# A decoder trunk's stages reordered across the two halves, with FFN operands and split mixer weights passed through DRAM

## Chip, core and metric

The kernel runs on one core of a Trainium2 chip. The time is the device time of one execution in microseconds, the median of several runs; lower is better. TensorE is shown as PE, VectorE as DVE, ScalarE as ACT, GpSimd as POOL, SyncE as SP.

## What is computed

One layer on a sequence of 2048 positions of width 1024, everything in float32:

```python
h = rmsnorm(x, norm_mix)
z_pool, z_cv, z_cg, z_u, z_v, z_gate = split(h @ w_in)      # 5632 columns
y_a = pool_mixer(z_pool)          # causal means over 2, 4, 8, 16 positions, then 128x256 products
y_b = conv_module(z_cv, z_cg)     # causal depthwise conv of 31 taps, layernorm, silu, product
y_c = sgu_mixer(z_u, z_v)         # gelu, layernorm, product along 128-position chunks, product
g = sigmoid(z_gate + b_gate)      # three gates of width 1024
x = x + (g0 * y_a + g1 * y_b + g2 * y_c) @ w_out
h = rmsnorm(x, norm_ffn)
a, val = split(h @ ffn_up)        # 2 x 2816 columns
x = x + (silu(causal_dwconv3(a)) * val) @ ffn_down
out = rmsnorm(x, norm_final)
```

## The kernel before

**Precision.** Every float32 operand of a product is split in two parts: `hi`, a rounded copy made on ScalarE, and `lo = x - hi`, made on VectorE. `mm3` makes three matmuls of 128x128 by 128x512 from them (hi.hi, hi.lo, lo.hi; lines 225 to 227). Nearly all of TensorE's work is this.

**Tiling.** The sequence is cut into four quarters of 512 positions (`NQ = 4`, `T = 512`), channels lie on the partitions, and a tile of one quarter is 128x512, 256 KB. An arena of 67 such tiles (`halves`) holds all data that moves; `half` takes one, `release` gives it back. PSUM has eight banks of 128x512.

**Stages.** Two quarters make a half, and each half runs: mix of its first quarter, mix of its second, the FFN's first product `ffn_up` for both quarters together, `down` of the first, `down` of the second. A mix is `mixers` plus `w_out`, 61 weight chunks and 1476 matmuls. `ffn_up` uses Strassen's scheme with seven products p1 to p7 for each of 22 index values (1848 matmuls): the two quarters and the two halves of the 1024 input channels make a 2x2 matrix of blocks, the gate and value columns of the weight make the other. Its moving operands are a11, a12, s2, s1, s3, a22, s4, each four tile pairs, 56 tiles in all; `first_sums` makes the first two during the last `w_out`, `second_sums` the others as `ffn_up` begins. `up_order` is the order of products by hand. `down` is two passes (`h`) of 22 steps (`k`) of 12 matmuls, each pass over half of the output channels.

**Weights.** `self.seq` lists the weight parts in order of use. `load` brings one from DRAM into `raw` (two buffers of 512 KB) on SP's queue, `ensure` splits it into `whi` and `wlo` (four buffers, `AHEAD = 4`) as soon as a chunk retires, with priority. A chunk serves 24 matmuls. For `ffn_up` the parts are `x1` (the plain block for p1, p2), `t2` and `t3` (differences that GpSimd makes from a pair of blocks in the double tile `both`, line 161) and `b22`.

**Order.** TensorE, SP and GpSimd follow the written order; VectorE and ScalarE are ordered by the framework's scheduler by priority. Each engine works its own list in order. `bg` is a list of small background steps (mostly the 31 taps of the convolution) that `drain` works off between chunks. The `acts` of the FFN and the residual `x1` go to DRAM on ScalarE's queue and come back on SP's; `queue_act` loads an act and splits it, once for each pass of `down`. During the second `down` of the first half the next quarter's x is loaded and its norm made (`next_x`, `norm_cols`).

## Time and profile before

| | us |
|---|---|
| median of 3 runs | 2829.61 (2827.94 to 2830.6) |
| the profiled run | 2830.14 |
| its span, first to last instruction | 2828.4 |
| TensorE busy | 2767.2 |
| VectorE busy | 1978.9 |
| ScalarE busy | 1167.3 |
| GpSimd busy | 424.9 |

Busy time of an engine is time in which at least one of its instructions is in work. Matmuls overlap, so TensorE's busy time says little of its rate; the number of matmuls that begin in a stretch does, together with the clock that was granted (1.00 is 2.4 GHz, 0.50 is 1.2 GHz).

### The profile page before, as it was taken

How to read it: one execution, taken by the hardware profiler on the slowest of the kernel's cores; microseconds unless marked ns; L12 is line 12 of the kernel's file. 1: busy time of each engine (PE TensorE's matmuls, PEld its weight loads, DVE VectorE, ACT ScalarE, POOL GpSimd, SP SyncE). 2: the span in 40 equal slices, each digit the busy share in tenths (PEclk: the TensorE clock that was granted, in tenths of full speed). 3: DMA queues.
4: the chain of work that ended last, by engine and by line, in shares of the span. 5: the costliest groups of instructions: out<-in, count | busy, mean ns of one | idle time of the engine just before them, and what ended most of it. 6: DMA issues, size and time to landing. Idle time of an engine off the chain costs nothing.

```text
span 2828.4 us, 32169 instructions
## 1 busy us (share of the span) xinstructions
PE 2767.2 (98%) x11938; PEld 2231.7 (79%) x11938; DVE 1978.9 (70%) x2980; ACT 1167.3 (41%) x1628; POOL 424.9 (15%) x326
## 2 busy tenths in 40 slices
PE   8999999999899999999999999999998999999998
PEld 7888888888688887787788888888886888877886
DVE  8995889658856565555689857896688556555565
ACT  4434324253544443445434343242534444434443
POOL 1000100000332332000200301000003332330020
PEclk9999999999899999999999999999998999999999
DMA  4224332333133233566432443323332233235564
GB/s 162 90 93 153 112 127 82 104 120 127 57 115 119 90 119 108 175 216 216 171 112 82 143 167 116 120 82 97 127 119 82 90 119 111 98 112 191 204 223 156
DMA packets 130013, 361.13 MB, mean 128 GB/s; under 512 B 14624, under 2 KB 16672, under 8 KB 129856
## 3 DMA queue, kind: packets, MB, share of 16 engines
q1 hardware_dynamic: 109296, 319.60, 33.8%
q10 hardware_dynamic: 18432, 32.51, 3.0%
q0 software_dynamic: 2128, 6.96, 0.6%
q8 instruction: 93, 1.52, 0.2%
q14 instruction: 64, 0.52, 0.1%
HBM read 318.65 MB, written 40.37 MB: 127 GB/s over the span
## 4 chain that ended last, share of the span: by engine, by line
PE 92%; DVE 3%; DMA 2%; POOL 1%; ACT 1%; issue 1%; SPq 0%; DVEq 0%; POOLq 0%; ACTq 0%
PE ps L226 30%; PE ps L227 30%; PE ps L225 30%; DVE h L268 1%; DMA both<-wts 1%; DVE wlo L193 1%; POOL tw L161 1%; DMA h<-act 1%; POOL h L355 0%; DMA h<-xT 0%; ACT whi L192 0%; PE ps L603 0%; ACT h L267 0%; PE ps L305 0%; PE ps L316 0%
## 5 line engine op out<-in xcount | busy, mean ns | idle before, releaser
L225 PE MATMUL ps<-h,whi 128*128 128x512 f32 x3648 | 1442.2, 395 | 27.1 <-ACT h L267 12.1
L226 PE MATMUL ps<-h,whi 128*128 128x512 f32 x3648 | 1442.1, 395 | 19.0 <-DVE h L268 18.5
L227 PE MATMUL ps<-h,wlo 128*128 128x512 f32 x3648 | 1439.0, 394 | 2.0 <-DVE wlo L193 1.9
L225 PEld LDWEIGHTS ps<-h,whi 128*128 128x128 f32 x3648 | 689.3, 189 | 192.1 <-ACT h L267 16.3
L226 PEld LDWEIGHTS ps<-h,whi 128*128 128x128 f32 x3648 | 689.1, 189 | 191.0 <-DVE h L268 33.8
L227 PEld LDWEIGHTS ps<-h,wlo 128*128 128x128 f32 x3648 | 689.9, 189 | 160.8 <-DVE wlo L193 4.2
L192 ACT CAST whi<-raw 128x1024 fp32r<-128x1024 f32 x376 | 394.2, 1050 | 891.0 <-PE ps L226 636.2
L193 DVE TENSOR_TENSOR wlo<-raw,whi 128x1024 fp32r<-128x1024 f32 x376 | 470.2, 1252 | 340.2 <-ACT whi L192 337.7
L444 DVE SCALAR_TENSOR_TENSOR h<-cbuf,params,h 128x512 f32<-128x512 f32 x480 | 340.6, 747 | 2.5
L193 DVE TENSOR_TENSOR wlo<-tw,whi 128x1024 fp32r<-128x1024 f32 x88 | 107.8, 1225 | 309.5 <-ACT whi L192 309.3
L161 POOL TENSOR_TENSOR tw<-both 128x512 f32<-128x512 f32 x88 | 122.9, 1396 | 1239.5 <-DMA both<-wts 1064.7
L268 DVE TENSOR_TENSOR h<-h,h 128x512 fp32r<-128x512 f32 x309 | 228.0, 764 | 68.0 <-ACT h L267 64.6
L267 ACT CAST h<-h 128x512 fp32r<-128x512 f32 x309 | 189.1, 619 | 183.9 <-DMA h<-act 75.3
L192 ACT CAST whi<-tw 128x1024 fp32r<-128x1024 f32 x88 | 92.4, 1050 | 212.7 <-POOL tw L161 119.5
L161 POOL TENSOR_TENSOR tw<-both,tw 128x512 f32<-128x512 f32 x88 | 156.5, 1778 | 3.4
L992 POOL TENSOR_TENSOR h<-h,h 128x512 f32<-128x512 f32 (+1 forms) x32 | 37.4, 1178 | 423.4 <-ACT h L982 422.9
L225 PE MATMUL ps<-whi,h 128*128 128x512 f32 x256 | 101.0, 395 | 0.0
L227 PE MATMUL ps<-whi,h 128*128 128x512 f32 x256 | 100.9, 394 | 0.0
L226 PE MATMUL ps<-wlo,h 128*128 128x512 f32 x256 | 100.7, 393 | 0.0
L355 POOL TENSOR_TENSOR h<-h,h 128x512 f32<-128x512 f32 x24 | 41.1, 1749 | 392.6 <-PE ps L227 375.4
L298 ACT ACTIVATE h<-h 128x512 f32<-128x512 f32 (+1 forms) x99 | 57.4, 609 | 39.1 <-DVE h L955 12.3
L299 DVE TENSOR_TENSOR h<-h,h 128x512 f32<-128x512 f32 (+1 forms) x82 | 58.9, 718 | 12.6 <-ACT h L298 9.5
(147 smaller groups left out, 1678.6 us busy)
## 6 DMA issues: line engine op xcount, KB each, us to landing
raw<-wts SPq DMA_DIRECT2D x376, 512.0 KB, 3.6
both<-wts SPq DMA_DIRECT2D x88, 512.0 KB, 4.5
h<-act SPq DMA_DIRECT2D x176, 256.0 KB, 4.1
act<-h ACTq DMA_DIRECT2D x88, 256.0 KB, 3.0
h<-xT SPq DMA_DIRECT2D x64, 256.0 KB, 5.4
x<-h ACTq DMA_DIRECT2D x32, 256.0 KB, 4.3
h<-x SPq DMA_DIRECT2D x32, 256.0 KB, 5.0
out<-h POOLq DMA_DIRECT2D x24, 256.0 KB, 2.7
```

Of the source, the lines that this page charges most:

```text
L161: sub = lambda o, a, b: self.nc.gpsimd.tensor_tensor(o, a, b, op=ALU.subtract)
L192: nc.scalar.copy(h, src)
L193: nc.vector.tensor_tensor(l, src, h.bitcast(F32), op=ALU.subtract)
L225: mm(out, l[0], r[0], start=start, stop=False)
L226: mm(out, l[0], r[1], start=False, stop=False)
L227: mm(out, l[1], r[0], start=False, stop=stop)
L267: self.nc.scalar.copy(hi, src)
L268: self.nc.vector.tensor_tensor(lo, src, hi.bitcast(F32), op=ALU.subtract)
L298: self.nc.scalar.activation(t, x, AF.Square)
L299: eng.tensor_tensor(s, s, t, op=ALU.add)
L355: nc.gpsimd.tensor_tensor(t, x[k], rstd, op=ALU.mult)
L444: nc.vector.scalar_tensor_tensor(acc, buf[:, k:k + T], w, acc, op0=ALU.mult, op1=ALU.add)
```

## The change

The stages run in another order: mix 0, mix 1, mix 2, `ffn_up` of the first half, `down(0)`, mix 3, `down(1)`, `ffn_up` of the second half, `down(2)`, `down(3)`.

The operands of `ffn_up` are made by a background job, `rows_job`: it loads x1 of both quarters, norms it, makes the seven blocks, splits them and stores them in DRAM. Jobs are generators; `tick` runs one step of each list between chunks, if the arena has room. `fetch_block` brings a block back. `spill` queues a store, which `flush` issues on SP one call later. The stores of acts and x1 go the same way, so none is issued by ScalarE.

The split weights of the mixers are stored in DRAM, those of odd chunks in mix 0 and of even ones in mix 1 (`put`), and from the next mix on the pair `hi`, `lo` is loaded (`get`) in place of the raw chunk and its split. `raw` has three buffers, the double tile is gone, and `b22` is loaded again by itself. `up_order` puts p4 and p3 of an index among the products of the next one. `down` keeps the 22 acts of a quarter, split, in the arena for both passes. The squares for the FFN's norm are added on GpSimd. GpSimd is ordered by the scheduler like VectorE and ScalarE. The final norms of the first three quarters are jobs too.

```diff
-NHALF = 67
-RAW = 2
+NHALF = 69
+RAW = 3
...
+def up_order(first=0, end=NPAIR):
+    out = [(p, first + i) for i in range(LAG) for p in ("p1", "p2")]
+    for i in range(first, end + 1):
+        n = i + LAG - 1 if i > first else end
+        out += [("p6", i), ("p4", i - 1), ("p5", i), ("p1", n), ("p7", i), ("p2", n), ("p3", i - 1)]
+    return [(p, i) for p, i in out if first <= i < end]
...
+        def mix(q):
+            return [(("w", "put", "get")[min(2, max(0, q + i % 2))], i) for i in range(ca)]
+        self.seq = mix(0) + mix(1) + mix(2) + up + down + mix(2) + down + up + down * 2
...
     def load(self):
...
+        elif what == "b22":
+            raw = self.wpool.tile([P, 1024], F32, name="raw", tag="raw", bufs=RAW)[:, 0:T]
+            self.nc.sync.dma_start(out=raw, in_=self.aps["wts"][i + NPAIR][:, T:])
         elif what == "t2":
-            raw = self.wpool.tile([P, 2, 1024], F32, name="both", tag="both", bufs=1)
+            raw = []
             for h in range(2):
-                self.nc.sync.dma_start(out=raw[:, h, :], in_=self.aps["wts"][i + h * NFF])
+                raw.append(self.wpool.tile([P, 1024], F32, name="raw", tag="raw", bufs=RAW))
+                self.nc.sync.dma_start(out=raw[h], in_=self.aps["wts"][i + h * NPAIR])
...
     def ensure(self, ahead=AHEAD):
-            if self.loaded < n and self.loaded - self.prepped < RAW and ahead > 1:
+            if self.loaded < n and self.loaded - self.prepped < 2 and ahead > 1 and not (
+                    self.loaded > self.prepped and self.seq[self.prepped][0] == "t3"):
                 self.load()
...
+                if what == "get":
+                    for t, d in zip((hi, lo), self.cache[i]):
+                        nc.sync.dma_start(out=t.bitcast(F32), in_=d)
+                    self.ready.append((hi, lo))
+                    self.prepped += 1
+                    continue
...
     def take(self, ahead=AHEAD):
         self.ensure(ahead)
+        got = self.ready.popleft()
+        what, i = self.seq[self.taken]
+        if what == "put":
+            for t, d in zip(got, self.cache[i]):
+                self.nc.sync.dma_start(out=d, in_=t.bitcast(F32))
...
+    def tick(self, n=1):
+        for _ in range(n):
+            for jobs in self.jobs:
+                if jobs and self.room() >= self.spare + jobs[0][1]:
+                    self.step(jobs)
...
+    def flush(self, n=1):
+        for _ in range(n):
+            for dst, keys, t, flag in self.due:
+                self.nc.sync.dma_start(out=dst, in_=t)
+                release(keys)
+                if flag:
+                    self.there[flag] = True
+            self.due, self.fresh = self.fresh, []
...
     def next_col(self, h, mid=None, at=(4,), ahead=AHEAD):
         ps = self.col(self.take(ahead), h, mid=mid, at=at)
         self.retire()
+        self.flush()
+        self.tick(self.pace)
...
     def w_out(...):
-            self.nc.scalar.dma_start(out=self.x1[q][j], in_=x1[j])
+            self.add_square(s[1], x1[j], nc.gpsimd, j == 0)
+            self.spill(self.x1[q][j], [keys[j]], x1[j])
...
+    def rows_job(self, st, q0, src, gname, rst, flags):
...
+        while not all(self.there[f] for f in flags):
+            yield 4
+        yield 4
+        kr, r = self.fetch(rst)
+        nxt = self.fetch([src[q][0] for q in (q0, q0 + 1)])
+        yield
+        yield
+        for k in range(H):
+            (k0, k2), (a0, b0) = nxt
+            yield 3
+            norm(a0, k, 0)
+            norm(b0, k, 1)
+            self.block(st, "a11", k, a0)
+            ks, s3 = self.half()
+            g.tensor_tensor(s3, a0, b0, op=ALU.subtract)
...
+            (k3,), (b1,) = self.fetch([src[q0 + 1][k + H]])
+            self.block(st, "s3", k, s3)
...
+            norm(b1, k + H, 1)
+            self.block(st, "a22", k, b1)
+            g.tensor_tensor(b0, b0, b1, op=ALU.add)
+            g.tensor_tensor(b1, b1, s3, op=ALU.subtract)
...
     def down(self, q, last, each, done, tail=None):
             for k in range(n):
-                self.queue_act(q, h, k + AHEAD)
+                if h == 0:
+                    self.queue_act(q, k + 2 * AHEAD)
...
+                if h == 0:
+                    acts[k] = self.queued.pop((q, k))
+                step(w, k, range(F4), slice(0, T), acts[k][1])
+                if h:
+                    release(acts[k][0])
+                    if not last:
+                        self.queue_act(q + 1, k)
...
     def build(self):
+        for q in range(3):
+            rows = next_rows(q + 1) if q < 2 else iter(range(4))
+            self.pace = 1 + (q == 2)
...
+                if q == 2 and got in (1, 2):
+                    self.need("f0")
+                    self.fetch_block("f0", BLOCKS[got - 1])
...
+                if q == 2 and j in (0, 2, 4):
+                    self.fetch_block("f0", BLOCKS[2 + j // 2])
...
+        rows = next_rows(3)
+        def each(h, k):
+            self.tick()
+            if h and k in (1, 6, 12, 16):
+                got["h"] = next(rows)
+        x = self.down(0, True, each, done(0, nc.gpsimd))
...
-        with tc.manual_schedule(engines={mybir.EngineType.PE, mybir.EngineType.SP, mybir.EngineType.Pool}):
+        with tc.manual_schedule(engines={mybir.EngineType.PE, mybir.EngineType.SP}):
```

`need` works off the jobs at once until the blocks named are stored; in the third mix it is called before the last eight products, in `down(1)` at step 10 of the second pass.

## Rows read from the trace of the kernel before

**Rows 1.** The page: busy time by engine; DMA total.
```profile
PE 2767.2 (98%) x11938; PEld 2231.7 (79%) x11938; DVE 1978.9 (70%) x2980; ACT 1167.3 (41%) x1628; POOL 424.9 (15%) x326
DMA packets 130013, 361.13 MB, mean 128 GB/s; under 512 B 14624, under 2 KB 16672, under 8 KB 129856
```

**Rows 2.** Stretches: busy us (starts) of PE, PEld, DVE, ACT, POOL; clock, DMA share, GB/s.
```profile
700.00:760.00 60.00, 49.51 (x184) 35.07 (x183) 55.50 (x84) 30.20 (x45) 21.27 (x13) 0.86 0.13 47
800.00:860.00 60.00, 60.00 (x261) 48.68 (x261) 35.98 (x60) 25.22 (x34) 19.83 (x13) 1.00 0.32 116
1100.00:1180.00 80.00, 75.46 (x315) 59.23 (x314) 43.45 (x67) 31.22 (x43) 12.43 (x8) 0.98 0.44 151
1280.00:1320.00 40.00, 35.91 (x145) 28.37 (x144) 21.49 (x27) 21.60 (x34) 4.72 (x3) 0.91 0.60 210
1360.00:1400.00 40.00, 33.62 (x133) 26.27 (x132) 30.85 (x34) 16.71 (x24) 13.59 (x8) 0.91 0.42 141
2100.00:2160.00 60.00, 49.56 (x184) 35.25 (x183) 53.35 (x74) 27.98 (x43) 26.09 (x16) 0.86 0.20 72
2520.00:2580.00 60.00, 54.95 (x224) 42.25 (x223) 30.73 (x45) 22.73 (x31) 12.47 (x8) 0.97 0.44 146
```

**Rows 3.** The chain that ended last: start us, us, what ran.
```profile
739.10 3.47 DVE h L268 x2
...
1106.43 5.04 DMA both<-wts
1112.99 4.79 POOL tw L161 x3
...
1287.88 5.50 DMA h<-xT
...
1373.09 11.49 POOL h L355 x7
```

**Rows 4.** Groups of instructions: count, busy us, mean ns, idle before and its cause.
```profile
L193 DVE TENSOR_TENSOR wlo<-raw,whi 128x1024 fp32r<-128x1024 f32 x376 | 470.2, 1252 | 340.2 <-ACT whi L192 337.7
L192 ACT CAST whi<-raw 128x1024 fp32r<-128x1024 f32 x376 | 394.2, 1050 | 891.0 <-PE ps L226 636.2 <-issue 120.7 <-PE ps L227 95.7
L268 DVE TENSOR_TENSOR h<-h,h 128x512 fp32r<-128x512 f32 x309 | 228.0, 764 | 68.0 <-ACT h L267 64.6 <-issue 3.1
L267 ACT CAST h<-h 128x512 fp32r<-128x512 f32 x309 | 189.1, 619 | 183.9 <-DMA h<-act 75.3 <-DVE h L652 57.9 <-DVE h L506 12.8
L161 POOL TENSOR_TENSOR tw<-both,tw 128x512 f32<-128x512 f32 x88 | 156.5, 1778 | 3.4
L161 POOL TENSOR_TENSOR tw<-both 128x512 f32<-128x512 f32 x88 | 122.9, 1396 | 1239.5 <-DMA both<-wts 1064.7 <-DVE h L765 102.3 <-DVE h L900 32.0
L782 DVE SCALAR_TENSOR_TENSOR h<-h,params,h 128x512 f32<-128x512 f32 x16 | 11.3, 745 | 0.0
```

**Rows 5.** The page's DMA issues: queue, count, size, median us to landing.
```profile
raw<-wts SPq DMA_DIRECT2D x376, 512.0 KB, 3.6
```

**Rows 6.** Stretches of 20 us with the highest DMA traffic, columns as in rows 2.
```profile
260.00:280.00 20.00, 20.00 (x88) 16.17 (x87) 13.82 (x20) 12.73 (x17) 0.00 (x0) 1.00 0.80 297
...
1260.00:1280.00 20.00, 20.00 (x88) 16.19 (x87) 10.40 (x14) 9.24 (x13) 1.31 (x1) 1.00 0.73 261
...
2720.00:2740.00 20.00, 20.00 (x88) 16.22 (x87) 16.79 (x11) 7.33 (x10) 11.98 (x13) 1.00 0.80 273
```

**Rows 7.** The middle of the second mix, columns as in rows 2.
```profile
380.00:530.00 150.00, 150.00 (x658) 121.98 (x657) 147.32 (x247) 55.20 (x85) 0.00 (x0) 1.00 0.31 99
```

**Rows 8.** Pool copies and products, 40 to 600 us: min/median/max, first and last start.
```profile
L495 ACT COPY h<-ps x8: 572/582/622, 107.1 to 473.2; 128x512 f32<-128x512 f32 x8
...
L506 DVE SCALAR_TENSOR_TENSOR h<-h,h x8: 681/684/687, 110.7 to 482.5; 128x512 f32<-128x512 f32 x8
```

**Rows 9.** SP's waits by cause: us in total, times, longest.
```profile
SPq L150 <- DVE wlo L193: 1474.1, 308, 14.7
```

**Rows 10.** SP in order of time: start us, us, what was issued.
```profile
1287.44 4.72 SPq L371 DMA_DIRECT2D h<-xT  x8
```

## What I expect of the change, before seeing it run

> **What bounds the kernel now.** I read the page's first part first. TensorE is busy for 2767 of 2828.4 us and VectorE for 1979; the DMA engines move 361 MB at a mean of 128 GB/s [rows 1]. So no work taken off VectorE or the DMA engines shortens the run by itself; only time in which TensorE stands still, or is slow, can be won. The busy share hides how much that is, because a matmul counts as busy while it waits for its operands to stream. I therefore counted matmul starts by stretch. A full stretch holds 261 starts in 60 us, 0.230 us each [rows 2]. The reader is to see that the short stretches are few and sit only where one stage hands over to the next: the two entries of the FFN's first product (184 starts in 60 us at a granted clock of 0.86, a mean of 2.4 GHz and half of it), its two ends, and two places in the second `down` of the first half. Between them, for hundreds of microseconds, the rate is full.
>
> The losses, starts missing times 0.230 us [rows 2]: entry of the first FFN, 261 - 184 = 77, 17.7 us; the same at the second, 17.7; end of the first, 348 - 315 = 33, 7.6; of the second, 261 - 224 = 37, 8.5; at 1280, 174 - 145 = 29, 6.7; at 1360, 174 - 133 = 41, 9.4. Together 67.6 us. What follows an idle stretch at a low clock is in these counts.
>
> The chain says what each place waits for [rows 3]. At the FFN's entry VectorE and ScalarE make the operand rows while TensorE waits for each. At the FFN's end it is the load of the next weight pair, then GpSimd's subtractions one after another. At 1287 the x of the next quarter is loaded, and act splits queue behind its squares. At 1373 seven GpSimd products of the next norm come in a row, with act splits behind them on ScalarE.
>
> Outside these places lie the start and the final norm's tail, which the change leaves alone. 2828.4 - 67.6 = 2760.8 us is the span if all six places close and nothing opens.
>
> **The change, part by part.** Matmuls: the counts of `mixers`, `strassen` and `down` are those of before; only some sums for a norm differ, under 1 us. Hence the whole effect lies in stalls.
>
> *FFN entry (gain 35.4, bounds 0 and 35.4).* `rows_job` makes the seven operands during the third mix and during `down(1)`, and they come back by DMA from the a11 block on, some 60 us ahead in the first half. The work does not vanish. Per half it is 16 norm products at 0.745, 28 splits at 0.619 on ScalarE and 0.764 on VectorE, and 16 sums on GpSimd at about 1.6, between its 1.4 and 1.8 [rows 4]: 33 us of VectorE, 17 of ScalarE, 26 of GpSimd, 77 in series. Its cover is 340 us of matmuls in the mix (1476 x 0.230) and 122 in `down(1)`. VectorE was full in the middle of a mix, 147 of 150 us [rows 7]. There, however, 61 weight splits of 1.25 us go (76 us of VectorE, 64 of ScalarE [rows 4]), as the third and fourth mix fetch them ready-made. In all 152 such splits and 88 act splits leave: 190 + 67 us of VectorE and 160 + 54 of ScalarE. That is worth nothing to the end but room.
>
> *FFN end (gain 16.1, bounds 0 and 16.1).* The two tiles of a pair now come from the three `raw` buffers, not from one double tile that stays full until `b22` is split; the next pair can load as soon as t3 is subtracted. A pair of 5.04 us [rows 3], 3.2 us of GpSimd and 2.3 of splits make 10.5 us; without p1 and p2 an index lasts 60 x 0.230 = 13.8 us. I leave 2 us for what still shows.
>
> *Inside the FFN.* t3's split must now wait for p4 of the index before, and p7 uses it two products, 5.5 us, later; before there were four products between them. The split takes 1.05 + 1.25 us [rows 4], leaving 3.2 us for whatever ScalarE and VectorE are in the middle of. Bounds: nothing, or 44 times the whole 2.3 us if nothing of it hides, 101 us; I take nothing, since one running instruction on each, at most about 1 us, fits.
>
> *`down` to mix.* The fourth quarter's norm is made in the second pass of `down(0)`, where acts stay resident: no act is loaded or split there, so the 16.1 us at 1280 and 1360 have no victim. But the norm now starts 6 steps (16.6 us) before the mix, and its eight GpSimd products alone take about 14 us (seven took 11.49 [rows 3]). Bounds 0 and 9.4, the old price of that chain; I take 4.
>
> *DMA.* Bytes go from 361 to about 566 MB: 122 stores of split weights (64 MB), 304 loads of 0.52 MB for 152 of the same (+80), 224 block moves (+59), x1 read again (+13), `b22` again (+12), fewer act loads (-23). Over the run that is 204 GB/s. The third mix carries the peak: 64 MB of weights, 15 of spilled blocks, 11 of fetched ones, about 11 of x, x1 and the rest, 101 MB in 340 us, 297 GB/s. That is just the fastest 20 us of before, 297 GB/s at a DMA share of 0.80 with TensorE at full rate [rows 6]. A weight is asked for three chunks, 16.6 us, ahead and lands in 3.6 for the first 0.5 MB, about 5 for two [rows 5], so some 11 us are in hand. They go in `w_out(2)`: behind the two chunks that retire together stand 2.1 MB of weights and 2.1 of s2, then 3.1 more, then 1.05 for the last chunk. These 8.4 MB take 23.5 us at the 358 GB/s that 261 at a share of 0.73 makes [rows 6], and 2.2 us of landing; the chunk is due 22.1 us after them: 3.6 us late. Bounds 0, and 12 at the bare 261 GB/s; I take 4.
>
> *The SP queue.* x1 and act stores move from ScalarE's queue to SP's, and with them all spills. SP works in order; it already stands waiting much of the time, 1474 us for weight splits on one line [rows 9], which costs nothing because raw loads are issued four to five chunks ahead. Now a spill that waits for a late split holds the next weight. `flush` puts one chunk between making and storing. Eight issues take 4.72 us [rows 10]; the third mix has some 256 (122 halves of weights, 134 of 0.26 MB), so about 151 of 340 us. How late VectorE runs: the eighth pool copy on ScalarE comes 9.3 us before its VectorE product [rows 8], inside the 11 us in hand, less the chunk. Bounds 0 and 154 (below); I take 2.
>
> Sum: 2760.8 + 4 (`w_out`) + 4 (norm) + 2 (FFN end) + 2 (SP) = 2772.8 us of span. The profiled run was 2830.1, 1.7 above its span and 0.5 above the median, so the forecast is 2774.
>
> **The rivals.** *DMA binds the third mix.* The mean of 297 GB/s is the best of before, and stores are mixed in. At 273 GB/s, another stretch at a share of 0.80 [rows 6], it takes 370 us, 30 more; at 261, 387, 47 more. Time 2804 to 2821. For it speaks that demand and best row coincide; against it that 0.80 is not 1.
>
> *The row jobs reach TensorE through SP: slower.* Place: the third mix and `down(1)`. Each spill waits for its split, each fetch for a free half, each norm for its fetch, and the next weight stands behind them on SP. If the 77 us chain of each half came out of the cover whole, it would cost 154 us: 2774 + 154 = 2928. It ends even when 44% of it shows (67.6 of 154), and slower beyond; with half showing, 2851. For it speaks the full VectorE in mid-mix [rows 7]; against it the 76 us of splits that leave that mix.
>
> The Trainium skill (DMA: Bandwidth & Descriptors, Anatomy of one DMA) says that a DMA's semaphore wait is served on the issuing sequencer before the transfer is dispatched, not by the DMA engines. SP's rows of waiting agree [rows 9]; by that rule alone this rival would be the likely one wherever a spill is late.
>
> *t3's slot eats the gain: no change.* If the split is late by 1.3 us at each of the 44 indices, 57 us return: 2774 + 57 = 2831. It begins where ScalarE and VectorE make it wait over 3.2 us. Against it: one instruction each is under that.
>
> **How the numbers follow.** Forecast 0.66, with its own range of 2758 to 2792; DMA-bound mix 0.15; row jobs in SP's way 0.11; t3's slot 0.08. About 0.2%, 5.7 us, is what a measurement of this kernel can tell from no change. Faster by more: 0.66 + 0.15 + 0.02 (t3 at a smaller price) = 0.83. Within: 0.04 of t3 and 0.01 of the row jobs, 0.05. Slower: 0.10 + 0.02 = 0.12. The range runs from 2754, six places closed and the scattered losses a little smaller, to 2820, the DMA-bound mix at its dearer end; the third and fourth cases stay outside, under 0.2.
>
> **What would show it.** Right: 261 starts per 60 us across both FFN entries, at a clock of 1.00; 356 weight splits instead of 508; VectorE near 1710 us, ScalarE near 950, DMA near 566 MB. In `w_out(2)` and at the entry of the fourth mix a wait of a few microseconds each, the first for a weight's DMA, the second for a norm's split. Wrong: TensorE waiting for DMA loads of weights through the third mix (first rival), SP rows waiting for splits ahead of them (second), or one wait per FFN index for the split made from `tw` (third).

## The result, and the profile after

The changed kernel takes 2791.98 us (median of 4 runs, 2789.69 to 2792.74) against 2830.11 us (median of 4, 2827.94 to 2830.63): ratio 0.9865, interval 0.9848 to 0.9882. That is 38 us less. The forecast was 2774, 56 us less; the time lies inside the range given, 18 us above its likeliest value and at the upper edge of the 2758 to 2792 that belonged to the forecast's own case. The profiled execution took 2792.74 us with a span of 2791.0 us, so the accounting below is made against that span.

First the page of the changed kernel, busy time by engine and the DMA total. It answers to [rows 1].

```profile
PE 2753.0 (99%) x11958; PEld 2231.2 (80%) x11958; DVE 1819.1 (65%) x2701; ACT 966.2 (35%) x1390; POOL 446.4 (16%) x363
DMA packets 203456, 566.71 MB, mean 203 GB/s; under 512 B 22784, under 2 KB 24832, under 8 KB 203296
```

The reader is to see that 201 us of ScalarE went, near the 217 that were forecast, but 160 us of VectorE where 269 were (it was put at 1710), and that the bytes are the 566 MB that were counted; none of these says anything of where 38 us came from. For that the starts are counted again by stretch, in the columns of [rows 2]. By the count of its matmuls, the third mix of this kernel runs from 704 to 1056, `ffn_up` of the first half to 1489, `down(0)` to 1612, the fourth mix to 1962, `down(1)` to 2086, and the second `ffn_up` to 2527.

```profile
704.00:1056.00 352.00, 348.66 (x1510) 282.11 (x1510) 218.25 (x364) 81.17 (x138) 37.65 (x23) 1.00 0.81 282
800.00:840.00 40.00, 37.47 (x164) 30.16 (x163) 37.52 (x76) 15.20 (x27) 10.92 (x6) 0.96 0.81 276
1060.00:1100.00 40.00, 37.86 (x163) 30.18 (x162) 24.95 (x41) 17.00 (x23) 15.68 (x12) 0.96 0.60 218
1440.00:1500.00 60.00, 60.00 (x261) 48.75 (x260) 43.28 (x63) 26.32 (x38) 11.61 (x8) 1.00 0.48 160
1489.00:1612.00 123.00, 123.00 (x533) 99.89 (x532) 66.19 (x82) 48.50 (x66) 17.99 (x12) 1.00 0.52 179
1720.00:1760.00 40.00, 38.17 (x166) 30.47 (x165) 39.19 (x75) 13.40 (x23) 0.00 (x0) 0.96 0.37 131
2000.00:2120.00 120.00, 113.47 (x480) 90.87 (x478) 79.21 (x91) 46.36 (x66) 31.72 (x21) 0.97 0.99 363
2080.00:2140.00 60.00, 52.01 (x206) 40.59 (x205) 32.73 (x44) 20.97 (x30) 16.78 (x12) 0.91 0.95 350
2090.00:2120.00 30.00, 23.47 (x91) 17.80 (x89) 19.97 (x28) 12.20 (x18) 11.35 (x8) 0.89 1.04 398
2470.00:2530.00 60.00, 60.00 (x261) 48.60 (x260) 44.20 (x62) 26.10 (x36) 11.77 (x8) 1.00 0.45 147
```

Both FFN ends, at 1489 and 2527, and the whole of `down(0)` now run at the full rate, 0.230 to 0.231 us a start. The first FFN entry (1060) has 163 starts where 174 fit, 2.5 us lost; the second (2080) 206 where 261 fit, 12.7 us. Two new short places stand in the middle of the third and fourth mix: 164 and 166 starts. A stretch like these with 16 small transposes among its matmuls holds 183 when nothing stops it (shown below in a kernel where it does), so 4.4 and 3.9 us are lost.

What TensorE waited for, in total, times, longest:

```profile
PE ps L291 <- ACT whi L208: 8.4, 3, 5.2
PE ps L394 <- DVE rs_y L360: 7.4, 4, 4.4
PE ps L291 <- DVE h L675: 4.4, 3, 2.5
```

Not shown are 7.4 us at the start, where the kernel before waits 6.9, and two small groups of 1.7 and 1.6. The weight split `whi` of line 208 is waited for at the two FFN entries (1.6 and 6.8 us), `h` of line 675 in the middle of the two mixes, and the norm's root `rs_y`, once 4.5 us at the very end, now costs 3.0 us more in three places (0.8, 0.5 and 1.7). No load of a weight is waited for in the third mix.

SP at the second entry, in order of time (start us, us, what was issued), around the first product of `ffn_up` at 2086:

```profile
2067.37 3.99 SPq L285 DMA_DIRECT2D h<-f1a  x8
...
2088.95 1.00 SPq L164 DMA_DIRECT2D raw<-wts  x2
2090.24 12.34 SPq L285 DMA_DIRECT2D h<-f1s  x16
```

The last store of the row job (line 275) goes out at 2065.5. Behind it five groups of eight block tiles of 256 KB (line 285; 10.5 MB in 35 us) stand around the first pair of weights that is to be subtracted (line 164). Sixteen loads take 12.34 us to issue, 0.77 each, where eight took 4.72 before, 0.59 each [rows 10]. The pair issued at 2088.95 reaches GpSimd at 2096.92; its four subtractions, 3 us for two, end at 2102.99, and ScalarE, in whose list other work stands ahead, splits at 2106.73: that is the wait for `whi`.

### The profile page after: what moved, and what is told of

Read it like the earlier page. It is cut to its first block, busy times and chain, and to the rows that moved or that the text cites. A ratio compares the mean times of both kernels' runs of the same rounds, so it can differ in the third digit from the quotient of the medians.

```text
span 2791.0 us, 32498 instructions
## 1 busy us (share of the span) xinstructions
PE 2753.0 (99%) x11958; PEld 2231.2 (80%) x11958; DVE 1819.1 (65%) x2701; ACT 966.2 (35%) x1390; POOL 446.4 (16%) x363
## 3 DMA queue, kind: packets, MB, share of 16 engines
q10 hardware_dynamic: 1152, 1.05, 0.1%
## 4 chain that ended last, share of the span: by engine, by line
PE 93%; DVE 4%; DMA 1%; issue 1%; ACT 0%; POOL 0%; SPq 0%; DVEq 0%; ACTq 0%; POOLq 0%
PE ps L293 31%; PE ps L291 31%; PE ps L292 31%; DVE h L514 2%; DVE h L338 0%; DMA h<-x 0%; PE ps L386 0%; DMA h<-act 0%; DVE wlo L209 0%; DVE h L572 0%; DVE h L548 0%; DMA params<-par 0%; PE ps L394 0%; PE ps L375 0%; DVE h L539 0%
## 5 line engine op out<-in xcount | busy, mean ns | idle before, releaser
L209 DVE TENSOR_TENSOR wlo<-raw,whi 128x1024 fp32r<-128x1024 f32 (+1 forms) x268 | 351.2, 1311 | 291.9 <-ACT whi L208 237.8
L208 ACT CAST whi<-raw 128x1024 fp32r<-128x1024 f32 (+1 forms) x268 | 262.1, 979 | 543.2 <-PE ps L292 387.8
L514 DVE SCALAR_TENSOR_TENSOR h<-cbuf,params,h 128x512 f32<-128x512 f32 x480 | 357.8, 783 | 2.4
L369 POOL TENSOR_TENSOR h<-h,h 128x512 f32<-128x512 f32 x38 | 55.9, 1470 | 1154.1 <-ACT h L368 1153.5
L337 ACT CAST h<-h 128x512 fp32r<-128x512 f32 x219 | 133.7, 620 | 294.7 <-DVE h L858 80.8
L171 POOL TENSOR_TENSOR tw<-raw 128x512 f32<-128x512 f32 x88 | 115.4, 1331 | 591.1 <-DMA raw<-wts 466.5
L338 DVE TENSOR_TENSOR h<-h,h 128x512 fp32r<-128x512 f32 x219 | 163.0, 760 | 70.5 <-ACT h L337 68.8
L701 ACT ACTIVATE h<-ps,params 128x512 f32<-128x512 f32 x96 | 65.7, 687 | 255.6 <-PE ps L293 255.5
L719 DVE TENSOR_TENSOR h<-ps,h 128x512 f32<-128x512 f32 x64 | 44.2, 690 | 163.2 <-PE ps L293 156.1
L171 POOL TENSOR_TENSOR tw<-raw,tw 128x512 f32<-128x512 f32 x88 | 129.4, 1470 | 3.4
L955 DVE TENSOR_TENSOR h<-h,ps 128x512 f32<-128x512 f32 x44 | 30.3, 688 | 130.3 <-ACT h L954 130.3
```

The source lines that it names most:

```text
L171: sub = lambda o, a, b: self.nc.gpsimd.tensor_tensor(o, a, b, op=ALU.subtract)
L208: nc.scalar.copy(h, src)
L209: nc.vector.tensor_tensor(l, src, h.bitcast(F32), op=ALU.subtract)
L337: self.nc.scalar.copy(hi, src)
L338: self.nc.vector.tensor_tensor(lo, src, hi.bitcast(F32), op=ALU.subtract)
L369: eng.tensor_tensor(s, s, t, op=ALU.add)
```

## The experiments

All ratios are against the kernel before, which ran on the same chip. It took 2828.12 to 2829.46 us beside these kernels and 2830.11 beside the changed one, so up to 2.0 us of each difference to the change that is given below belongs to the chips. Against its own runs of the kernel before, the change saves 38.1 us, e1 42.8, e2 41.0, e3 27.3, e5 43.4, e6 39.2, e7 27.3, e9 32.6, e10 55.4, e11 45.0, and e12 loses 0.6. By the intervals only e3, e7, e10 and e12 are clear of the change; for the others the windows of the profiled runs have to decide. How far a window varies by itself can be seen in kernels that leave its place alone: 800 to 840 holds 156 starts in e2, 161 in e6, 173 in e9; 1060 to 1100 holds 163 in e6 and 169 in e2 and e9; 2080 to 2140 holds 206 in the changed kernel, 210 in e5 and 213 in e2.

**e1: spread the traffic at the two entries.** Blocks are fetched some products later, and the x1 of `down(1)` is stored one tile per product, not all at once.

```diff
-            self.fetch_rest("f0", m, (0, 0))
+            self.fetch_rest("f0", m, (3, 8))
...
-        for dst, key, t in zip(self.x1[1], *x):
-            self.spill(dst, [key], t)
+        later_x = {m: (dst, [key], t) for m, (dst, key, t) in enumerate(zip(self.x1[1], *x))}
...
-            self.fetch_rest("f1", m, (0, 2, 8))
+            self.fetch_rest("f1", m, (3, 6, 10))
+            if m in later_x:
+                self.spill(*later_x[m])
```

> The blocks left over at the entry of each FFN product are loaded a few products later (a22 and s4 at products 3 and 8 instead of both at 0; s3, a22, s4 at 3, 6, 10 instead of 0, 2, 8), and the eight stores of x1 at the second entry go out one per product. No work is left out. Theory: TensorE stands still there because 16 to 24 block tiles stand ahead of the weights on SP's queue; the losses of 2.8 and 12.7 us at the two entries fall below 5 together and the time to about 2782. Rival: the second entry is late because the call of need holds SP until the last row spills are made; then the 12.7 us stay within 3 us and the time is 2789 or more.

Measured: 2785.97, ratio 0.9854 (0.9837 to 0.987), 6.0 us below the change, between the 2782 of the theory and the 2789 of the rival. The second entry in e1, columns as in rows 2:

```profile
2075.00:2125.00 50.00, 43.82 (x175) 34.64 (x174) 30.21 (x38) 18.90 (x26) 15.03 (x11) 0.90 0.95 353
```

The first entry is full (262 starts in 1050 to 1110). The second still loses 42 starts of 217, 9.7 us, at a DMA share of 0.95. Spreading what follows 2086 moves some 3 us of the 12.7 at most, as e2 and e5 differ there by 1 to 2 without a change of theirs; most of the loss stays.

**e2: the final norm's job later.** One number, so that the final norm of the first quarter runs later in the fourth mix.

```diff
-        self.add(self.later(4, self.final(0, x, got[0])))
+        self.add(self.later(30, self.final(0, x, got[0])))
```

> The final norm of the first quarter starts 26 chunks later in the fourth mix. No work is left out. Theory: its GpSimd products and DMA issues slow the convolution's taps on VectorE (18 taps took 22.9 us, 12.6 without it), and TensorE pays 4.4 us for that in the middle of the mix; the wait for the gated product's split goes, and the time falls to about 2788. Rival: VectorE is full in the middle of a mix anyway; the wait stays over 3 us and the time at 2791 to 2793.

Measured: 2787.73, 0.9856 (0.9842 to 0.9871); 4.3 us below the change, as the theory had it, and 1720 to 1760 is full. First e2's window, with the 16 transposes in it:

```profile
1720.00:1760.00 40.00, 40.00 (x183) 32.72 (x182) 30.72 (x51) 12.82 (x21) 0.00 (x0) 1.00 0.45 158
```

The cause is in VectorE's order of time, the taps of the convolution (line 514) shortly after the mix begins. In the changed kernel:

```profile
1647.35 16.32 DVE L514 SCALAR_TENSOR_TENSOR h<-cbuf,params,h 128x512 f32<-128x512 f32 x8
```

GpSimd in the same stretch of the changed kernel:

```profile
1647.89 3.05 POOL L1092 TENSOR_TENSOR h<-h,h 128x512 f32<-128x512 f32 x2 [31.24 <-ACT h L1082]
1650.89 1.13 POOL L1093 DMA_DIRECT2D out<-h  x2
1652.03 2.54 POOL L1092 TENSOR_TENSOR h<-h,h 128x512 f32<-128x512 f32 x2
1654.49 1.12 POOL L1093 DMA_DIRECT2D out<-h  x2
```

And VectorE in e2, where GpSimd does nothing there:

```profile
1648.42 10.68 DVE L514 SCALAR_TENSOR_TENSOR h<-cbuf,params,h 128x512 f32<-128x512 f32 x16
```

Eight taps in 16.32 us beside GpSimd, sixteen in 10.68 without: a tap of 0.67 us became 2.04 in the mean. Not all eight are slow. Three last 0.74 us, two 1.78 and three 3.7; here are one of each of the slow kinds:

```profile
1648.01 1.78 DVE L514 SCALAR_TENSOR_TENSOR h<-cbuf,params,h 128x512 f32<-128x512 f32 x1
```

```profile
1651.41 3.71 DVE L514 SCALAR_TENSOR_TENSOR h<-cbuf,params,h 128x512 f32<-128x512 f32 x1
```

The first ends when the GpSimd product beside it does, within 0.2 us. The second begins between two DMA issues of GpSimd and lasts through one issue, two products and the next issue. The 11 us of VectorE lost here are missed 70 us later, where VectorE has no slack (39.19 busy of 40). Whether TensorE feels it depends on the order of VectorE's list: e3 (below) has five such taps too, the longest 3.71 us, and the middle of its fourth mix is full.

**e5: the first row job later.** The same for the job that makes the FFN's operands in the third mix.

```diff
-                self.add(self.rows_job("f0", 0, self.x1, "nffn", self.rst[:2], [("rst", 0), ("rst", 1)]))
+                self.add(self.later(30, self.rows_job("f0", 0, self.x1, "nffn", self.rst[:2], [("rst", 0), ("rst", 1)])))
```

> In the third mix the row job starts 30 steps, 15 chunks, later, after the convolution's taps and the value rows. No work is left out. Theory: its VectorE and GpSimd work among the taps makes the gated product's split late, 4.4 us in the middle of that mix; the wait goes, and the time is about 2788 unless the later stores delay the last blocks. Rival: VectorE is full there without the job; the wait stays over 3 us and the time at 2791 to 2794.

Measured: 2784.73, 0.9848 (0.9833 to 0.9862), 7.3 us below the change. The window of e5 that lost 4.4:

```profile
800.00:840.00 40.00, 40.00 (x183) 32.62 (x182) 38.32 (x73) 12.60 (x21) 1.58 (x1) 1.00 0.50 180
```

Full; GpSimd has 1.58 us of work in it instead of 10.92, VectorE is as busy as before. But e5 takes more out of the stretch than GpSimd's sums: the row job's own work on VectorE goes too. The taps (line 514) and the operand splits (line 338) from 750 to 840, first in the changed kernel, then in e5:

```profile
L514 DVE SCALAR_TENSOR_TENSOR h<-cbuf,params,h 128x512 f32<-128x512 f32 x42 | 33.5, 835 | 0.0
L338 DVE TENSOR_TENSOR h<-h,h 128x512 fp32r<-128x512 f32 x22 | 17.8, 815 | 2.8 <-ACT h L337 2.5
```

```profile
L514 DVE SCALAR_TENSOR_TENSOR h<-cbuf,params,h 128x512 f32<-128x512 f32 x76 | 54.2, 758 | 0.1
L338 DVE TENSOR_TENSOR h<-h,h 128x512 fp32r<-128x512 f32 x6 | 4.1, 683 | 0.0
```

The longer taps are worth 42 x 0.088 = 3.7 us of VectorE against the mean of before, 747 ns; the splits that go are worth 13.7. Which of the two makes the 4.4 us was not separated. The gain beyond 4.4 is scattered; the first entry has 169 starts in 1060 to 1100, but so has e2, which changes nothing there.

**e3: no split weights in DRAM.** Each mix loads and splits its weights itself.

```diff
-            return [(("w", "put", "get")[min(2, max(0, q + i % 2))], i) for i in range(ca)]
+            return [("w", i) for i in range(ca)]
```

> All mixes load raw weights and split them, nothing is put into or fetched from DRAM ready-made: 508 splits again, DMA down by about 144 MB. Theory: the ready-made weights are the room on VectorE in which the row job runs; without them the third and fourth mix stall for 10 to 40 us each, 2810 to 2870. Rival: what is left of the loss is DMA; with 100 us less of DMA time at the mixes the FFN entry and the mixes get faster, 2775 to 2785.

Measured: 2801.51, 0.9905 (0.989 to 0.9919), 9.5 us above the change, the direction that the theory had, but less than its size. E3's mid-mix window and its new wait:

```profile
800.00:860.00 60.00, 54.09 (x224) 42.44 (x223) 58.12 (x107) 34.13 (x63) 15.26 (x7) 0.91 0.60 192
```

```profile
PE ps L292 <- DVE h L548: 4.5, 3, 2.1
```

VectorE is full there (58.12 of 60), and 46 of the 270 starts that fit (261 and 9 for the transposes) are missing: 10.6 us, where the change loses 4.4. Another 3.2 us go at 720 to 740, where the norm's root is waited for 2.9 us (0.8 in the change). The middle of the fourth mix loses nothing (312 starts in 1720 to 1790). So the freed VectorE time is worth something to the end, some 6 us in the middle of the third mix: room that the row job uses. The second FFN entry is not better (about 11 us): the weight traffic of the mixes is not what fills the engines there.

**e4: the rows at need.** The row job in the third mix gets no steps of its own until `need` calls it.

```diff
-            self.pace = 1 + (q == 2)
+            self.pace = q < 2
```

> The background steps of the third mix do not run between its chunks; the row job runs as one piece when its blocks are called for, after the last gates. No work is left out. Theory of the prediction: the chain of 77 us of VectorE, ScalarE and GpSimd, with its loads, comes out in series less the 11 us of weights in hand: 60 to 100 us more, 2850 to 2890. Rival: the three engines overlap within the job, VectorE's 33 us set its length, and 20 to 35 us come out: 2812 to 2827.

Measured, one run: 2857.95, 66 us above the change and inside the 60 to 100 of the theory. E4's window, and its greatest wait of TensorE:

```profile
1000.00:1080.00 80.00, 16.74 (x60) 11.98 (x59) 45.76 (x60) 20.23 (x34) 23.72 (x15) 0.59 0.81 294
```

```profile
PE ps L291 <- DMA whi<-wc: 63.2, 2, 62.7
```

With the cover gone the 77 us chain does come out: SP stands in stores that wait for splits (29.1 us for ScalarE's, 12.8 for VectorE's between 990 and 1080), and the next ready-made weight stands behind them. The second rival's mechanism is real, and its price is near what was worked out; in the changed kernel the mix covers it.

**e6: the second row job quicker.** Three steps per product in `down(1)` instead of two, so that its stores end sooner.

```diff
-            self.tick(2)
+            self.tick(3)
```

> In down(1) three background steps run per step of the loop instead of two, so that the row job of the second half is further when its blocks are called for. No work is left out. Theory: SP is held about 10 us by the job's last stores, and the blocks and the first pair of weights come that much late; the 12.7 us at the second FFN entry fall below 5 and the time to 2783 to 2785. Rival: the DMA engines are full there (share 0.97 to 1.04 for 120 us), so the bytes set the time; the loss stays over 10 us and the time at 2790 to 2793.

Measured: 2788.89, 0.9863 (0.9848 to 0.9877), 3.1 us below the change (1.1 by the savings above); neither theory's range holds it. Windows of e6:

```profile
2010.00:2070.00 60.00, 55.07 (x229) 43.30 (x228) 42.30 (x48) 23.77 (x34) 16.01 (x10) 0.97 0.93 334
2080.00:2140.00 60.00, 59.00 (x253) 47.04 (x252) 37.38 (x46) 23.64 (x32) 17.86 (x12) 1.00 0.91 332
```

The entry is nearly full (253 of 261), and `down(1)` loses 7.4 us that it did not lose before. The loss moved into `down(1)`, with the row job's stores; that it follows the bytes is only argued here, and e11 tests it.

**e7: the old order of products** on the new buffers.

> The FFN's products run in the order of the kernel before, with the three raw buffers and the b22 loads of the change. No work is left out. Theory: the buffers closed the gap at the end of the FFN, and the later slot of t3 costs nothing: 2789 to 2795, no wait at either end. Rival one: the order closed it; both ends lose 6 to 8 us, 2804 to 2808. Rival two: the new order costs time at every index; 2770 to 2785.

Its edit, cut to its core:

```diff
-        out += [("p6", i), ("p4", i - 1), ("p5", i), ("p1", n), ("p7", i), ("p2", n), ("p3", i - 1)]
+            out += [("p6", i), ("p5", i), ("p7", i), ("p1", n), ("p4", i), ("p2", n), ("p3", i)]
```

Measured: 2800.84, 0.9906 (0.9889 to 0.9922), 8.9 us above the change, where 2789 to 2795 was expected. The second entry in e7:

```profile
2085.00:2160.00 75.00, 61.88 (x248) 47.78 (x248) 38.53 (x56) 27.09 (x38) 16.07 (x12) 0.93 0.76 278
```

The ends stay closed (257 starts of 261 in 1460 to 1520, and 260 in 2500 to 2560), so the three `raw` buffers in place of the double tile closed them, not the order. What the new order is worth lies elsewhere: the second entry has 248 starts in 75 us against 271 in the changed kernel, 5.3 us, and TensorE waits 5.5 us in four places for a copy on ScalarE (line 959) before a bank is written again, which the changed kernel does not show; the kernel before has such waits too, 3.7 us in four places (line 889). The late split for t3 that the third rival feared shows no cost: with t3 in its old place the kernel is slower.

**e9 and e12: the acts loaded and split twice.** Both drop the resident acts; e9 asks for an act eight steps ahead, e12 four, as the kernel before did. The edit of e12 (e9 has `2 * AHEAD`):

```diff
-                if h == 0:
-                    self.queue_act(q, k + 2 * AHEAD)
+                n_h, n_k = (h, k + AHEAD) if k + AHEAD < NFF else (h + 1, k + AHEAD - NFF)
+                if n_h < 2:
+                    self.queue_act(q, n_k, n_h)
+                elif not last:
+                    self.queue_act(q + 1, n_k, 0)
...
```

> Acts are loaded and split once for each pass of down, eight steps ahead, as before the change; 88 more loads and splits. No work is left out. Theory: resident acts removed the victim of the fourth quarter's norm; in the second pass of down(0) act splits queue behind that norm again and 6 to 16 us come back: 2798 to 2808. Rival: the norm is spread better than before, and eight steps ahead are enough; within 2 us of 2792.

> As the run with acts loaded twice, but four steps ahead instead of eight, the distance of the kernel before. No work is left out. Theory: eight steps (22 us) ahead cover the norm's chain of GpSimd products and four (11 us) do not, so the loss of the kernel before comes back in the second pass of down(0): 6 to 16 us there, 2801 to 2812. Rival: the norm, cut into four calls over 15 steps, is not in the way of act splits at either distance; no loss in down(0), and the time within 3 us of 2795.

Measured: e9 2795.5, 0.9884 (0.9869 to 0.9899); e12 2830.03, 1.0002 (0.9993 to 1.0012). Windows of e9:

```profile
1600.00:1625.00 25.00, 25.00 (x109) 20.26 (x109) 11.90 (x18) 9.16 (x14) 9.89 (x7) 1.00 0.54 201
2000.00:2100.00 100.00, 93.95 (x397) 73.51 (x396) 75.06 (x91) 47.44 (x72) 21.64 (x13) 1.00 1.02 383
```

Windows of e12:

```profile
1600.00:1625.00 25.00, 22.45 (x84) 17.47 (x83) 12.96 (x16) 11.42 (x17) 13.70 (x10) 0.86 0.40 147
2000.00:2100.00 100.00, 77.51 (x268) 56.20 (x267) 64.07 (x79) 39.29 (x60) 22.50 (x14) 0.88 0.89 320
```

Up to 1600 `down(0)` is at the full rate in both kernels (542 starts in 125 us from 1475), and e9 stays so to its end, as the changed kernel does (109 starts from 1600 to 1625). E12 does not: 25 starts are missing there, at the end of the second pass, 5.8 us, just under the theory's 6 to 16. In front of it stands what stood at 1373 in the kernel before, GpSimd's norm products in a row, and behind them on ScalarE the last two act splits:

```profile
1595.76 12.75 POOL L425 TENSOR_TENSOR h<-h,h 128x512 f32<-128x512 f32 x8 [37.49 <-DVE h L360]
```

```profile
1609.17 1.12 ACT L337 CAST h<-h 128x512 fp32r<-128x512 f32 x2
```

So an act that is loaded again in the second pass is a victim of that norm at the old distance, and none at eight steps: at this place residency and distance each do the job. The other place, 1280 before, has no counterpart in either kernel. Both lose in `down(1)` besides. E9 loses 37 starts of 434 there, 8.5 us, and gets some back at the entry behind it; e12 loses 166, 38 us, about the whole gain of the change, for acts whose splits come late (15.6 us of waits for ScalarE's part between 1960 and 2140, 10.5 for VectorE's). Where the DMA engines are near full, distance counts most: the same bytes asked four steps ahead or eight differ by 34.5 us, most of it in `down(1)`.

**e11: half the stores of the second row job.** This kernel leaves out half of the columns of each block that the second row job stores (7.3 MB in `down(1)`); they hold ones, written during the first FFN, so its output is not the layer's. SP issues as many instructions in `down(1)` as before, in the same order.

```diff
-            self.spill(d, [key], s.bitcast(F32), (st, name, k))
+            h = T // 2 if st == "f1" else T
+            self.spill(d[:, 0:h], [key], s[:, 0:h].bitcast(F32), (st, name, k))
```

> Left out: the second half of the columns of every block that the second row job stores, 7.3 MB of stores in down(1); those columns are filled with ones during the first FFN, when the DMA engines have room, so the second half's output is not the layer's. The number and the order of SP's instructions in down(1) stay. Theory now: the DMA engines are full from the row job to the second FFN's entry, and bytes set the loss there; it falls from 12.3 to under 7 us, the time to 2782 to 2787. Rival: SP's order and the stores' waits for splits set it; the loss stays over 10 us and the time at 2789 to 2793.

Measured: 2784.19, 0.9844 (0.9828 to 0.9861), 7.8 us below the change. The entry in e11, and SP at the loads of a11:

```profile
2090.00:2120.00 30.00, 25.41 (x104) 20.23 (x103) 16.23 (x25) 12.96 (x17) 11.01 (x8) 0.94 1.01 370
```

```profile
2060.30 5.57 SPq L285 DMA_DIRECT2D h<-f1a  x8
```

The loss at the entry falls from 12.7 to about 6, and SP reaches the loads of a11 at 2060.30 instead of 2067.37. With the number of issues held, it is the bytes that matter: 7.3 MB fewer bring SP there 7 us sooner. No weight is waited for at this entry any more; what is left is mostly one wait of 4.6 us for a copy on ScalarE (line 952), whose cause stays open.

**e10: what the others point to**, together: e1, e2 and e5, fetches in `down(1)` four steps apart instead of three, one block more fetched during `ffn_up`, and x1 stored two products later than in e1. The lines that are e10's own, without those of e1, e2 and e5:

```diff
-            if h and k in (10, 13, 16, 19):
+            if h and k in (10, 14, 18):
...
-                self.fetch_block("f1", BLOCKS[(k - 10) // 3])
+                self.fetch_block("f1", BLOCKS[(k - 10) // 4])
...
-            self.fetch_rest("f1", m, (0, 2, 8))
+            self.fetch_rest("f1", m, (1, 3, 6, 10))
```

> The late row job of the third mix, the late final norm of the fourth and the spread loads at both FFN entries together; at the second entry s1 moves into the FFN too (products 1, 3, 6, 10 for the last four blocks) and the stores of x1 start two products in. No work is left out. Theory: the four places are separate, so the savings of 7.3, 4.3 and 6.0 us nearly add; no wait in the two mixes or at the first entry, under 6 us at the second: 2773 to 2779. Rival: they share one cause, the full DMA engines, and do not add; 2782 to 2786.

Measured: 2773.83 (2773.14 to 2777.23), 0.9807 (0.9793 to 0.9822), better than both kernels and 18.2 us below the change; e1, e2 and e5 alone saved 6.0, 4.3 and 7.3, together 17.6. Against their own runs of the kernel before that is 17.2 for e10 and 12.9 for the three, and e10 has two edits more, so that the savings simply add is not shown; that the places close together is. Its second entry:

```profile
2080.00:2120.00 40.00, 38.21 (x148) 27.34 (x147) 26.95 (x33) 17.72 (x24) 14.34 (x10) 0.96 0.92 331
```

Only the second entry still loses, 27 starts from 2080 to 2160, 6.2 us. The first entry (175 starts in 1060 to 1100) and both mid-mix places are full.

## Why the prediction was right, and where 18 us went

**The six places: right.** They lost 67.6 us [rows 2]. Of these both ends and the two places in `down` are at zero, and the entries fell from 17.7 each to 2.5 and 12.7: 52.4 us came back. The mechanism named for the ends, single buffers in place of the double tile, is shown by e7. For `down` it is shown in part: I said that no act is loaded there, so nothing is delayed. At the later place e12 bears that out, as acts loaded again at the old distance lose 5.8 us behind the norm, but e9 shows that asking eight steps ahead does as well there as residency. What closed the earlier place, at 1280, stays open: e9 and e12 load the acts twice and lose nothing there. The moved x loads and norm of the next quarter are the nearest candidate and were not tried alone.

**The residues: the step that failed.** I took 4 for DMA in `w_out(2)`, 4 for the norm before the fourth mix, 2 for the FFN's ends and 2 for SP's queue, 12 in all. Neither of the first two showed: TensorE waits for no weight in the third mix (282 GB/s and a share of 0.81, about what [rows 6] showed to be free), and for a norm's root, 0.5 us, at the fourth mix. Nor did the ends. The mis-sized terms are DMA and SP, 4 + 2 taken, 15.2 measured at the FFN's entries; in other words, the entry's gain was taken whole, 35.4, and 20.2 came. All losses together are 30.2 us (2791.0 - 2760.8) where 12 were taken. I had counted the bytes of the third mix alone, the longer stage, and called it the peak; the same 15 MB of stores, their fetches, the acts and the weights of `down(1)` go into 124 us instead of 340, and 2000 to 2120 ran at 363 GB/s and a share of 0.99. E6 moves that loss within the full stretch, e11 halves it by taking bytes away, e1 and e10 by spreading them. The first rival was right in kind and wrong in place, and a hundred microseconds at a share of 0.99 cost 12.7, not 30. That the time still lies inside the range owes something to luck: the range reaches to 2820 for a third mix bound by DMA, which did not come.

The second rival's sign, SP waiting for splits in front of it, does show in `down(1)` of the changed kernel (1962 to 2087), in 25.2 us of waiting for the row job's two kinds of splits; in the third mix it is 8.3:

```profile
SPq L275 <- ACT h L337: 14.7, 11, 2.2
SPq L275 <- DVE h L338: 10.5, 17, 1.2
```

How much of the 12.7 us is due to this waiting was not separated. It does not set the loss alone, as e10 has 25.1 us of the same waits in `down(1)` and loses half as much. The rival's break-even was also worked out wrong: from 2774 the old time comes back when 56 us of the 154 show, 36%, not 67.6 and 44%, as the 12 us of residues had already been paid.

The Trainium skill (DMA: Bandwidth & Descriptors, Anatomy of one DMA) has a DMA's wait served on the issuing sequencer before dispatch. The trace agrees: in e4 the spills' waits stand on SP, 41.9 us between 990 and 1080, and TensorE waits 62.7 us for a weight load behind them. By that rule the second rival should have been likely wherever a spill is late.

**"Worth nothing to the end but room": too strong.** The time freed on VectorE was not free of what GpSimd does beside it. In the middle of both mixes VectorE is full, as [rows 7] said it would be, and the new GpSimd work, sums of a row job in the one and the final norm's products and stores in the other, makes VectorE's taps longer. TensorE loses 8.3 us in these two places, of which I had none. In the fourth mix e2 shows the cause; in the third the job's own work on VectorE is the rival. The lengthening shows in the groups of the changed kernel, shapes kept apart (line, count | busy us, mean ns | idle before and its cause):

```profile
L514 DVE SCALAR_TENSOR_TENSOR h<-cbuf,params,h 128x512 f32<-128x512 f32 x480 | 357.8, 783 | 2.4
L209 DVE TENSOR_TENSOR wlo<-raw,whi 128x1024 fp32r<-128x1024 f32 x224 | 289.2, 1292 | 252.0 <-ACT whi L208 197.8 <-DMA wc<-wlo 24.2 <-DMA raw<-wts 9.2
L209 DVE TENSOR_TENSOR wlo<-raw,whi 128x512 fp32r<-128x512 f32 x44 | 62.0, 1409 | 39.9 <-ACT whi L208 39.9
L979 DVE SCALAR_TENSOR_TENSOR h<-fhalo,params,h 128x1 f32<-128x1 f32 x88 | 46.6, 530 | 1.6
```

The same taps, `b22` splits and one-column operations in the kernel before:

```profile
L444 DVE SCALAR_TENSOR_TENSOR h<-cbuf,params,h 128x512 f32<-128x512 f32 x480 | 340.6, 747 | 2.5
L193 DVE TENSOR_TENSOR wlo<-both,whi 128x512 fp32r<-128x512 f32 x44 | 30.2, 685 | 10.8 <-ACT whi L192 10.8
L765 DVE SCALAR_TENSOR_TENSOR h<-fhalo,params,h 128x1 f32<-128x1 f32 x88 | 20.9, 238 | 0.2
```

The 356 weight splits are there, 224 + 44 and 88 made from `tw`. But a tap's mean rose from 747 to 783 ns, a raw split's from 1252 [rows 4] to 1292, that of `b22` (128x512) from 685 to 1409, and a one-column operation's from 238 to 530. Over their counts that is 17 + 9 + 32 + 26 = 84 us of the 109 by which VectorE's 1819 exceeds my 1710. The last two lie inside the FFN, beside GpSimd's subtractions, where VectorE has room; the taps lie in the mixes, where it has none. E2 takes GpSimd's work out of the one stretch, e5 the whole row job out of the other, and the loss goes.

The Trainium skill (SBUF — State Buffer, Who interferes with whom) says that a VectorE instruction with two inputs in SBUF contends with a GpSimd instruction that reads SBUF, as its second input comes through a read interface that the two share. The trace agrees: a tap has two such inputs, and eight of them took 16.32 us beside GpSimd's products, sixteen 10.68 without.

**Small terms.** The norm's roots are waited for 3.0 us more, in three places. I put the matmuls that differ at under 1 us: there are 24 more small ones and 4 fewer large. Sixteen small ones lengthen a 40 us stretch from 174 to 183 starts, so one takes about (40 - 167 x 0.230)/16 = 0.10 us, and 24 x 0.10 - 4 x 0.23 = 1.5 us (an estimate, as 16 of the 24 are of another shape, 128x1). The start has 133 matmuls in its first 40 us instead of 136, 0.7 us.

Summed: 2760.8 + 2.5 + 12.7 (entries) + 4.4 + 3.9 (mid-mix) + 3.0 + 1.5 + 0.7 = 2789.5 of 2791.0. The other 1.5 us stay open; the second FFN has 1466 starts in 2160 to 2500 where the kernel before has 1470, 0.9 us, which may hold some of them. The same sum for e10, 2760.8 + 6.2 + 3.1 + 1.5 + 0.5, gives 2772.1 for a span of 2771.4.

**The third rival** (t3's slot) did not show: full rate inside both FFNs, and e7 with the old order is slower, not faster.

## What to carry to other kernels

Work that is moved into the background is priced by the shortest stage that has to carry it, not by the longest: count its bytes against each stage's own length, and spread loads or ask for them further ahead where the DMA share comes near 1. Before GpSimd is given work to free VectorE, look at what VectorE does in those microseconds; a chain of two-input operations beside it can lose time (11 us in the fourth mix here), and the bill may come tens of microseconds later. When one step of a schedule is shifted, look for the loss in the next stage before calling it gone.

## What the runs showed of the hardware that was not expected

A VectorE operation on a single column, 128x1, has a mean of 530 ns here against 238 before. At 2099.97, beside GpSimd's subtractions, one took 1.22 us; at 2103.84, after they had ended, the next took 0.22. A tap of 128x512 beside one GpSimd product took 1.78 us against 0.74. So both sizes lost about 1.0 us: in these cases the contention costs time by the instruction and not by its size, and short operations suffer most in proportion. A tap that met a train of GpSimd instructions was not let go after the first of them: it lasted 3.7 us, where one product takes 1.3.

The DMA engines moved 363 GB/s over 120 us, loads and stores mixed, at a share of 0.99, 398 GB/s over 30 us (2090 to 2120), and in e9 383 GB/s over 100 us. I had reckoned with 358 as what a full share gives, and with 297 as the best that was seen.

The time that SP takes to issue a load of 256 KB is not fixed: 0.50 us (8 in 3.99) at 2067, 0.69 (8 in 5.54) at 2083, 0.77 (16 in 12.34) at 2090. The DMA share was 0.99 to 1.05 in all three stretches, so a full share alone does not explain it, and the cause stays open.
